# Attention of a two-layer decoder trunk: half of each unit's softmax scaling as row-scalar products on GpSimd

## The chip, the cores and the metric

One core of one Trainium2 chip. The metric is the device time of one launch in microseconds; of the kernel before there are three runs, with a median of 1051.75 us (1051.14 to 1052.2). Engines are called by their short names in the profile: PE (TensorE; PEld is its weight load), DVE (VectorE), ACT (ScalarE), POOL (GpSimd) and SP (the queue that issues most transfers).

## The reference

Layer one is a gated MLP with a spatial mix inside chunks of 128 positions. It also yields one K and one V for the second layer, which is attention over a sliding window of 128 positions, with 16 query heads that share 4 key/value heads, a sink logit per head and a linear position bias (cut to what the change touches):

```
logits = einsum('btkgd,bskd->bkgts', qb, kb) + alibi
logits = where(valid, logits, -inf)
m      = maximum(max(logits, -1), sink)
p      = exp(logits - m)
denom  = sum(p, -1) + exp(sink - m)
o      = einsum('bkgts,bskd->btkgd', p, vb) / denom
y      = (o * silu(z)) @ w_out
```

Every array is float32: x is (1, 1024, 1024), there are 8 blocks of 128 positions, and heads are 64 wide.

## The kernel before, in words

Large products are made in three passes: each operand is split into a rounded part `hi` and a rest `lo`, and PE adds hi*hi, hi*lo and lo*hi (L169 to L171). For a weight of the second layer, ACT makes `whi` (L109, or L105) and DVE makes `wlo` (L110, or L106) from a raw tile that a transfer has brought; `whi` and `wlo` have two buffers each. A weight that carries a gain is split in two halves, k=0 and then k=1, and PE's product reads the half that it needs.

Attention runs over the 1024 positions in two halves of 512 (`attn(0)`, `attn(1)`). Each half has 8 *units*, one for each pair of key/value heads p (0 or 1) and each block b of 128 positions; a unit has eight heads. In this text "unit 5_0" is block 5, pair 0. A unit goes through these steps:

- `scores(gp)`, for the first four heads (gp=0) and then for the last four (gp=1): eight matmuls (L1050) into two banks of PSUM; on DVE a predicated copy per bank (L1055) that folds the window, and one custom operation per head (L1061) that adds the bias and leaves the row's extreme in `mx`; on ACT one exponential per head (L1065) that leaves the row sum in `dn`.
- `normalise`: one reciprocal of `dn` for eight heads (L1070) and one multiplication of all eight heads' probabilities `pr` by it (L1071), both on DVE.
- `transposes`: PE transposes the eight heads of `pr` (L1078), ACT copies them to `pc` (L1079), POOL cuts the two triangles of the window out of it with two selects (`pp` L1082, `pc` L1083; a sequence's first block has only the second).
- `values`: PE multiplies `pc` and `pp` with V (L1097, L1099), DVE multiplies by the gate z (L1103) and splits the result (L105, L106).

The loop of `attn` staggers the units: in step i stand the scores of the first four heads of unit i, the values of unit i-2, the transposes of unit i-1, the scores of the last four heads of unit i and its normalisation. Between these, `more()` lets PE do pieces of other work: the products for K, V, q and z of the second half (`qz`, `pk`, `pv`) beside `attn(0)`, and the rest of z and the output product of the first half (`ob`) beside `attn(1)`. When a group of four q products is complete, ACT and DVE empty its four banks (L971 and L972, two halves per bank), and the banks are then used again.

Within an engine the instructions run in one fixed order. A list scheduler sets it when the kernel is built, from the program's order and its own estimate of when operands are ready, so a change at one place can move neighbours too.

Of the kernel before, what the change touches and what calls it, by code (L numbers as in the profile page):

```python
# [12 lines left out]
ALU = mybir.AluOpType  # L13

P = 128
# [35 lines left out]
def tile_yoco(  # L51
# [19 lines left out]
    nc = tc.nc  # L71
# [9 lines left out]
    def bank(tag, name):  # L81
        return psum.tile([P, 512], F32, tag=tag, name=name)
# [425 lines left out]
    def uz_layer():  # L508
# [149 lines left out]
        for q in range(len(quads) + 1):  # L658
# [39 lines left out]
            if zz:  # L698
                spatial(g, 0, 0)
                spatial(g, 0, 1)  # L700
                if not last:
                    finish(g, 0, 0)
            else:
                normalise(g)
# [22 lines left out]
    def post_gain(src, name):  # L727
        g = const.tile([P, D], F32, tag="gpost", name=name)
        nc.sync.dma_start(out=g, in_=src.partition_broadcast(P))
        return g  # L730
# [291 lines left out]
    class Unit:  # L1022
# [6 lines left out]
        def scores(self, gp):  # L1029
            b, p, q = self.b, self.p, self.q  # L1030
            bs_ = slice((b % 4) * P, (b % 4 + 1) * P)
            w0 = 0 if b > 0 else P
            if gp == 0:
                pr = bp.tile([P, 1088], F32, tag="pr", name=f"pr{self.id}", bufs=2)
                self.pr = pr = pr[:, 0:8 * (P + 1)].rearrange("p (a b) -> p a b", a=8)
                self.mx = bp.tile([P, 8], F32, tag="mx", name=f"mx{self.id}", bufs=2)
                self.dn = bp.tile([P, 8], F32, tag="dn", name=f"dn{self.id}", bufs=2)
                nc.vector.tensor_copy(pr[:, :, P].rearrange("p (c a b) -> p c a b", c=2, a=2),
                                      snk[:, 2 * p:2 * p + 2].rearrange("p a (c b) -> p c a b", c=2))
            pr, mx, dn = self.pr, self.mx, self.dn  # L1040
            pss = []
            for par in range(2):
                pss.append(bank("s", f"s{self.id}_{gp}{par}").rearrange("p (g s) -> p g s", g=2))
            ks = slice(b * P - P + w0, (b + 1) * P)

            for g in range(2):
                m = p * 4 + gp * 2 + g
                for par in range(2):
                    for k, w in enumerate((kh, kl)):
                        nc.tensor.matmul(pss[par][:, g, w0:256], lhsT=q[par][:, m, bs_], rhs=w[par][:, p, ks],  # L1050
                                         start=g + k == 0, stop=g + k == 2, skip_group_check=True)
            for par in range(2):
                ps = pss[par]
                c = ps[:, :, P:256]
                nc.vector.copy_predicated(c, mrg.bitcast(U32).unsqueeze(1).broadcast_to([P, 2, P]),  # L1055
                                          ps[:, :, 0:P] if b > 0 else neg.unsqueeze(1).broadcast_to([P, 2, P]))
                kv = 2 * p + par
                for g in range(2):
                    gg = 2 * gp + g
                    i = 4 * gp + 2 * par + g  # L1060
                    nc.vector.tensor_tensor_reduce(pr[:, i, 0:P], c[:, g], bias[:, gg], -(4.0 ** -kv),  # L1061
                                                   snk[:, kv, gg:gg + 1], ALU.add, ALU.min, mx[:, i:i + 1])

            for i in range(4 * gp, 4 * gp + 4):
                nc.scalar.activation(pr[:, i], pr[:, i], AF.Exp, bias=mx[:, i:i + 1], scale=-1.0,  # L1065
                                     accum_out=dn[:, i:i + 1])

        def normalise(self):
            dn, pv = self.dn, self.pr[:, :, 0:P]
            nc.vector.reciprocal(dn, dn)  # L1070
            nc.vector.tensor_tensor(pv, pv, dn.unsqueeze(2).broadcast_to([P, 8, P]), ALU.mult)  # L1071

        def transposes(self):
            self.pc = pc = st.tile([P, 8, P], F32, tag="xt", name=f"pc{self.id}")
# [136 lines left out]
    gp = post_gain(b_post, "gpb")  # L1211
# [82 lines left out]
```

## Time and profile before

| | us |
|---|---|
| median of the runs | 1051.75 |
| the profiled execution's own time | 1051.56 |
| its span | 1049.8 |
| outside its span | 1.76 |
| PE busy | 1039.2 |
| DVE busy | 731.9 |
| ACT busy | 577.2 |
| POOL busy | 195.2 |

The span is the time from the program's first to its last instruction on the profiled core; the execution's own time is longer by what lies around it. In timelines a row holds start, duration, engine, line, operation, the tiles written and read, shapes, the count of merged instructions, and in brackets the idle time before the row and what ended it.

### The profile page before, as it was taken

To read this page: it belongs to the slowest core of one execution; us is meant where nothing else is said; L and a number is where in the kernel's file an instruction comes from. 1 tells how busy PE (TensorE), PEld (TensorE's weight loads), DVE (VectorE), ACT (ScalarE), POOL (GpSimd) and SP (SyncE) were. 2 spreads that over 40 slices of the span, in tenths; PEclk is the share of its full clock that TensorE was granted. 3 is DMA by queue.
4 is the path that set the end of the run, shared out by engine and by line. 5 is a ranking of instruction groups with operands and counts; after the bars stand their busy time and mean duration, and the time that the engine had idled before them with its cause. 6 is when DMAs were issued, how large, how long until landed. Compare 5 with 4: busy or idle time off the path is not lost.

```text
span 1049.8 us, 13661 instructions
## 1 busy us (share of the span) xinstructions
PE 1039.2 (99%) x4994; PEld 854.8 (81%) x4994; DVE 731.9 (70%) x1244; ACT 577.2 (55%) x989; POOL 195.2 (19%) x153
## 2 busy tenths in 40 slices
PE   9999999999999999999999999999999999999997
PEld 7888788888888888888888888888888777877776
DVE  6997466867768668677697587665247776667763
ACT  6683444555465565555444464654466665786631
POOL 0300003253342542530200000100001111011120
PEclk9999999999999999999999999999999999999999
DMA  8877252334333333347897642532222121211363
GB/s 310 271 282 269 101 177 88 116 105 143 124 121 116 132 124 117 108 137 272 322 352 270 201 160 93 200 102 86 95 81 71 51 81 61 81 61 61 121 220 120
DMA packets 80899, 157.56 MB, mean 150 GB/s; under 512 B 5824, under 2 KB 32704, under 8 KB 80832
## 3 DMA queue, kind: packets, MB, share of 16 engines
q1 hardware_dynamic: 76176, 147.75, 41.2%
q10 hardware_dynamic: 4656, 8.94, 2.4%
q8 instruction: 39, 0.64, 0.3%
q14 instruction: 28, 0.23, 0.1%
HBM read 125.21 MB, written 31.46 MB: 149 GB/s over the span
## 4 chain that ended last, share of the span: by engine, by line
PE 93%; DVE 4%; ACT 1%; issue 0%; DMA 0%; POOL 0%; DVEq 0%; POOLq 0%; ACTq 0%
PE ob L169 6%; PE ub L169 6%; PE ub L171 6%; PE ob L171 6%; PE ob L170 6%; PE ub L170 6%; PE qz L169 5%; PE qz L171 5%; PE qz L170 5%; PE uc L169 3%; PE uc L171 3%; PE uc L170 3%; PE s L1050 3%; PE sp L614 3%; PE vb L170 2%; PE vb L171 2%
## 5 line engine op out<-in xcount | busy, mean ns | idle before, releaser
L110 DVE SCALAR_TENSOR_TENSOR wlo<-raw_w,gn,whi 128x512 fp32r<-128x512 f32 x80 | 58.7, 758 | 62.2 <-ACT whi L109 62.0
L169 PE MATMUL qz<-n_hi,whi 128*128 128x512 f32 x256 | 101.0, 394 | 0.4 <-DVE q_lo L972 0.4
L171 PE MATMUL qz<-n_hi,wlo 128*128 128x512 f32 x256 | 100.0, 391 | 1.2 <-DVE wlo L110 1.2
L170 PE MATMUL qz<-n_lo,whi 128*128 128x512 f32 x256 | 99.8, 390 | 0.0
L109 ACT ACTIVATE whi<-raw_w,gn 128x512 fp32r<-128x512 f32 x80 | 54.9, 716 | 54.2 <-PE qz L170 35.0
L1065 ACT ACTIVATE pr<-pr,mx 128x129 f32<-128x129 f32 x128 | 50.0, 393 | 40.1 <-DVE mx L1061 40.0
L169 PEld LDWEIGHTS qz<-n_hi,whi 128*128 128x128 f32 x256 | 48.0, 188 | 16.6 <-issue 6.5
L105 ACT ACTIVATE uzhilo_g<-f 128x1024 fp32r<-128x1024 f32 x31 | 32.9, 1060 | 48.6 <-PE uc L171 42.7
L171 PEld LDWEIGHTS qz<-n_hi,wlo 128*128 128x128 f32 x256 | 48.0, 188 | 12.3 <-DVE wlo L110 2.1
L170 PEld LDWEIGHTS qz<-n_lo,whi 128*128 128x128 f32 x256 | 48.1, 188 | 9.3
L106 DVE TENSOR_TENSOR uzhilo_g<-f,uzhilo_g 128x1024 fp32r<-128x1024 f32 x31 | 39.0, 1257 | 19.9 <-ACT uzhilo_g L105 19.9
L209 ACT ACTIVATE uz_slots<-ub 128x512 f32<-128x512 f32 x48 | 28.3, 590 | 42.4 <-PE ub L171 39.0
L169 PE MATMUL ub<-T,whi_g 128*128 128x512 f32 x128 | 50.7, 396 | 0.0
L169 PE MATMUL ub<-T,uzhilo_g 128*128 128x512 f32 x128 | 50.5, 395 | 0.0
L171 PE MATMUL ub<-T,wlo_g 128*128 128x512 f32 x128 | 49.9, 390 | 0.0
L171 PE MATMUL ub<-T,uzhilo_g 128*128 128x512 f32 x128 | 49.9, 390 | 0.0
L170 PE MATMUL ub<-T,uzhilo_g 128*128 128x512 f32 x128 | 49.8, 389 | 0.0
L170 PE MATMUL ub<-T,whi_g 128*128 128x512 f32 x128 | 49.8, 389 | 0.0
L169 PE MATMUL uc<-T,uzhilo_g 128*128 128x512 f32 x124 | 48.9, 395 | 0.0
L170 PE MATMUL uc<-T,uzhilo_g 128*128 128x512 f32 x124 | 48.3, 389 | 0.0
L171 PE MATMUL uc<-T,uzhilo_g 128*128 128x512 f32 x124 | 48.3, 389 | 0.0
L105 ACT ACTIVATE whi_g<-raw_uz 128x1024 fp32r<-128x1024 f32 (+1 forms) x31 | 26.5, 854 | 36.7 <-PE ub L170 15.6
(332 smaller groups left out, 3071.4 us busy)
## 6 DMA issues: line engine op xcount, KB each, us to landing
raw_uz<-in_wuz_in_dram SPq DMA_DIRECT2D x32, 512.0 KB, 3.4
raw_w<-in_wqz_dram SPq DMA_DIRECT2D x32, 512.0 KB, 3.5
td<-uz_slots SPq DMA_DIRECT2D x56, 256.0 KB, 2.2
orawP2a<-td SPq DMA_DIRECT2D x28, 512.0 KB, 4.0
raw<-in_wv_in_dram SPq DMA_DIRECT2D x17, 512.0 KB, 4.8
vg<-vd SPq DMA_DIRECT2D x8, 1024.0 KB, 5.4
orawP2b<-in_wo_a_dram SPq DMA_DIRECT2D x16, 512.0 KB, 7.7
vraw<-in_wv_in_dram SPq DMA_DIRECT2D x13, 512.0 KB, 4.4
```

Of the source, the lines that this page charges most:

```text
L105: nc.scalar.activation(hi, src, AF.Copy)
L106: nc.vector.tensor_tensor(lo, src, hi.bitcast(F32), ALU.subtract)
L109: nc.scalar.activation(hi, src, AF.Copy, scale=g)
L110: nc.vector.scalar_tensor_tensor(lo, src, g, hi.bitcast(F32), ALU.mult, ALU.subtract)
L169: nc.tensor.matmul(out, lhsT=a_hi, rhs=b_hi, start=start, stop=False, skip_group_check=True)
L170: nc.tensor.matmul(out, lhsT=a_hi, rhs=b_lo, start=False, stop=False, skip_group_check=True)
L171: nc.tensor.matmul(out, lhsT=a_lo, rhs=b_hi, start=False, stop=stop, skip_group_check=True)
L209: nc.scalar.activation(out, a, AF.Copy)
L614: nc.tensor.matmul(psv[:, n], lhsT=d["vg"][:, 4 * j + n, i * P:(i + 1) * P], rhs=d["wc"], start=True, stop=True)
L1050: nc.tensor.matmul(pss[par][:, g, w0:256], lhsT=q[par][:, m, bs_], rhs=w[par][:, p, ks], start=g + k == 0, stop=g + k == 2, skip_group_che ...
L1065: nc.scalar.activation(pr[:, i], pr[:, i], AF.Exp, bias=mx[:, i:i + 1], scale=-1.0, accum_out=dn[:, i:i + 1])
```

## The change

After the scores of the last four heads are issued, a reciprocal of the first four heads' sums is made on DVE (new L1053), and four POOL instructions each multiply one head's 128x128 probabilities by its column of `dn`, in place (new L1055). `normalise` (now L1070 to L1075) does the last four heads alone, as one reciprocal of four columns and one multiplication of four heads. All lines behind the new ones are four higher than before.

```
+            if gp == 1:
+                nc.vector.reciprocal(dn[:, 0:4], dn[:, 0:4])
+                for i in range(4):
+                    nc.gpsimd.tensor_scalar(pr[:, i, 0:P], pr[:, i, 0:P], dn[:, i:i + 1], None, ALU.mult)
...
         def normalise(self):
-            dn, pv = self.dn, self.pr[:, :, 0:P]
+            dn, pv = self.dn[:, 4:8], self.pr[:, 4:8, 0:P]
             nc.vector.reciprocal(dn, dn)
-            nc.vector.tensor_tensor(pv, pv, dn.unsqueeze(2).broadcast_to([P, 8, P]), ALU.mult)
+            nc.vector.tensor_tensor(pv, pv, dn.unsqueeze(2).broadcast_to([P, 4, P]), ALU.mult)
```

The new order differs from the old at several places on DVE and ACT, and on PE at one: of the eight score matmuls of the first four heads of unit 3_0, four now stand behind twelve `qz` matmuls instead of ahead of them.

The first place to look at is DVE behind the normalisation of unit 0_1, where four banks of q products (`qz1_0_0` to `qz1_0_3`) are emptied; `q1_hi` and `q1_lo` are the two halves written from a bank, `s1_1` are the next unit's scores. Before:

```order
L1070 RECIPROCAL dn0_1_6367<-dn0_1_6367 128x8
L1071 TENSOR_TENSOR pr0_1_6365<-pr0_1_6365,dn0_1_6367 128x8x128
L972 SCALAR_TENSOR_TENSOR q1_hi_5837<-qz1_0_1_6208,qsc_4951,q1_hi_5837 64x512
L972 SCALAR_TENSOR_TENSOR q1_hi_5837<-qz1_0_2_6209,qsc_4951,q1_hi_5837 64x512
L972 SCALAR_TENSOR_TENSOR q1_hi_5837<-qz1_0_3_6210,qsc_4951,q1_hi_5837 64x512
L972 SCALAR_TENSOR_TENSOR q1_lo_5838<-qz1_0_1_6208,qsc_4951,q1_lo_5838 64x512
L972 SCALAR_TENSOR_TENSOR q1_lo_5838<-qz1_0_2_6209,qsc_4951,q1_lo_5838 64x512
L972 SCALAR_TENSOR_TENSOR q1_lo_5838<-qz1_0_3_6210,qsc_4951,q1_lo_5838 64x512
```

The same place in the changed kernel:

```order
L1074 RECIPROCAL dn0_1_6387<-dn0_1_6387 128x4
L1075 TENSOR_TENSOR pr0_1_6385<-pr0_1_6385,dn0_1_6387 128x4x128
L972 SCALAR_TENSOR_TENSOR q1_hi_5837<-qz1_0_1_6223,qsc_4951,q1_hi_5837 64x512
L972 SCALAR_TENSOR_TENSOR q1_hi_5837<-qz1_0_2_6224,qsc_4951,q1_hi_5837 64x512
L1059 COPY_PREDICATED s1_1_00_6524<-mrg_4944,s1_1_00_6524 128x2x128
L972 SCALAR_TENSOR_TENSOR q1_lo_5838<-qz1_0_1_6223,qsc_4951,q1_lo_5838 64x512
L972 SCALAR_TENSOR_TENSOR q1_hi_5837<-qz1_0_3_6225,qsc_4951,q1_hi_5837 64x512
L972 SCALAR_TENSOR_TENSOR q1_lo_5838<-qz1_0_2_6224,qsc_4951,q1_lo_5838 64x512
L1065 ISA pr1_1_6520,mx1_1_6521<-s1_1_00_6524,bias_4942,snk_4953 128x128
L1065 ISA mx1_1_6521 128x1
L972 SCALAR_TENSOR_TENSOR q1_lo_5838<-qz1_0_3_6225,qsc_4951,q1_lo_5838 64x512
```

The multiplication ahead of the eviction is half as wide, the last operation on the bank `qz1_0_1` has moved one place up against the other evictions, and one predicated copy and one custom operation of unit 1_1 now stand among them. ACT's order has the matching swap (its half of `qz1_0_1` ahead of its half of `qz1_0_3`).

The second place is DVE at the scores of the last four heads of unit 4_0 (`s4_0_10`, `s4_0_11`), between the two halves of the weight split `wlo37`. Before:

```order
L110 SCALAR_TENSOR_TENSOR wlo37_7048<-raw_w37_6947,gn_80,whi37_7047 128x4x128
L1055 COPY_PREDICATED s4_0_10_7073<-mrg_4944,s4_0_10_7073 128x2x128
L1055 COPY_PREDICATED s4_0_11_7074<-mrg_4944,s4_0_11_7074 128x2x128
L110 SCALAR_TENSOR_TENSOR wlo37_7048<-raw_w37_6947,gn_80,whi37_7047 128x4x128
L1061 ISA pr4_0_7019,mx4_0_7020<-s4_0_10_7073,bias_4942,snk_4953 128x128
```

In the changed kernel:

```order
L110 SCALAR_TENSOR_TENSOR wlo37_7088<-raw_w37_6987,gn_80,whi37_7087 128x4x128
L1059 COPY_PREDICATED s4_0_10_7113<-mrg_4944,s4_0_10_7113 128x2x128
L1053 RECIPROCAL dn4_0_7061<-dn4_0_7061 128x4
L1059 COPY_PREDICATED s4_0_11_7114<-mrg_4944,s4_0_11_7114 128x2x128
L110 SCALAR_TENSOR_TENSOR wlo37_7088<-raw_w37_6987,gn_80,whi37_7087 128x4x128
L1065 ISA pr4_0_7059,mx4_0_7060<-s4_0_10_7113,bias_4942,snk_4953 128x128
```

The new reciprocal, which releases the four products on POOL, stands two instructions ahead of the second half of `wlo37`.

The third place is POOL from unit 4_0 to unit 6_0. Before, it holds the selects alone:

```order
L1082 AFFINE_SELECT pp4_0_7184<-pc4_0_7171 128x1024
L1083 AFFINE_SELECT pc4_0_7171<-pc4_0_7171 128x1024
L1082 AFFINE_SELECT pp5_0_7300<-pc5_0_7287 128x1024
L1083 AFFINE_SELECT pc5_0_7287<-pc5_0_7287 128x1024
L1082 AFFINE_SELECT pp6_0_7413<-pc6_0_7400 128x1024
L1083 AFFINE_SELECT pc6_0_7400<-pc6_0_7400 128x1024
```

In the changed kernel:

```order
L1055 TENSOR_SCALAR pr4_0_7059<-pr4_0_7059,dn4_0_7061 128x128 x4
L1055 TENSOR_SCALAR pr5_0_7166<-pr5_0_7166,dn5_0_7168 128x128 x4
L1086 AFFINE_SELECT pp4_0_7229<-pc4_0_7216 128x1024
L1087 AFFINE_SELECT pc4_0_7216<-pc4_0_7216 128x1024
L1055 TENSOR_SCALAR pr6_0_7277<-pr6_0_7277,dn6_0_7279 128x128 x4
L1086 AFFINE_SELECT pp5_0_7350<-pc5_0_7337 128x1024
L1087 AFFINE_SELECT pc5_0_7337<-pc5_0_7337 128x1024
L1055 TENSOR_SCALAR pr7_0_7405<-pr7_0_7405,dn7_0_7407 128x128 x4
L1086 AFFINE_SELECT pp6_0_7468<-pc6_0_7455 128x1024
L1087 AFFINE_SELECT pc6_0_7455<-pc6_0_7455 128x1024
```

Four products of a unit now stand ahead of the two selects of the unit before it, so a select can wait for products that came first.

## The prediction

> **What bounds the kernel now.** I read the page's first lines, then the stretch in which attention runs, then what PE waited for. The columns of the second row are length, then busy time and count for each engine.
>
> ```profile
> span 1049.8 us, 13661 instructions
> PE 1039.2 (99%) x4994; PEld 854.8 (81%) x4994; DVE 731.9 (70%) x1244; ACT 577.2 (55%) x989; POOL 195.2 (19%) x153
> ...
> 769.00:1005.00 236.00, 235.56 (x1251) 184.46 (x1250) 170.42 (x485) 157.62 (x418) 36.14 (x32) 1.00 0.23 72
> ...
> PE qz L169 <- DVE q_lo L972: 0.4, 1, 0.4
> ```
>
> PE is busy in 1039.2 of 1049.8 us, and in the 236 us from 769 to 1005, which hold every instruction that the change touches, it is idle for 236.00 - 235.56 = 0.44 us. That is one wait, for DVE's `q_lo` (L972). The change takes no matmul away, and PE's granted clock is already 1.00 there. So the most that it can gain is 0.44 us, 0.04%. About 0.2%, 2.1 us, is what a measurement of this kernel can tell from no change. The question is only whether the change makes PE wait.
>
> **What is removed and what is added.** Rows by line (count, then busy us and mean ns), then rows of single instructions:
>
> ```profile
> L1071 DVE TENSOR_TENSOR pr<-pr,dn 128x1024 f32<-128x1024 f32 x16 | 19.6, 1224 | 0.5
> 920.59 0.68 DVE L106 TENSOR_TENSOR q_lo<-z,q_hi 128x512 fp32r<-128x512 f32 x1
> L586 POOL TENSOR_SCALAR_AFFINE_SELECT wc<-wc x8: 292/298/8106, 38.9 to 412.0; 128x128 f32<-128x128 f32 x8
> L1284 POOL MEMSET const-float32-0.0<- 128x1 f32 x1 | 0.1, 103 | 0.3 <-issue 0.3
> L206 POOL TENSOR_TENSOR f<-raw_uz 128x512 f32<-128x512 f32 x15 | 20.1, 1338 | 127.6 <-DMA raw_uz<-in_wuz_in_dram 85.5 <-DVE uzhilo_g L106 42.1
> ```
>
> DVE loses half of sixteen multiplications: 1.22 us becomes about 0.68, the duration of a multiplication-like operation on 512 columns with both inputs in SBUF. That frees 16 x 0.54 = 8.6 us of DVE. Sixteen more reciprocals at 0.20 us (first row below) give 3.2 back. None of this is on PE's path except where PE waits for DVE. POOL gains 64 products of 128x128, which this trace does not have. Its nearest row is the select of the same shape with one input, 0.298 us at the median; the far ends are 0.10 us, a memset of one column, and 1.34 us, an addition on four times the columns. I take 0.30, with the gap of 0.07 that stands between two selects below: four products take 4 x 0.30 + 3 x 0.07 = 1.4 us.
>
> **The one wait goes.** DVE's rows at the first place that the change's section shows, then one of ACT's, then the matmuls of PE that begin in the last three of the four banks:
>
> ```profile
> 831.98 0.20 DVE L1070 RECIPROCAL dn<-dn 128x8 f32<-128x8 f32 x1 [0.91 <-ACT pr L1065]
> 832.21 1.22 DVE L1071 TENSOR_TENSOR pr<-pr,dn 128x1024 f32<-128x1024 f32 x1
> 833.47 2.06 DVE L972 SCALAR_TENSOR_TENSOR q_hi<-qz,qsc,q_hi 64x512 fp32r<-64x512 f32 x3
> 835.56 0.76 DVE L972 SCALAR_TENSOR_TENSOR q_lo<-qz,qsc,q_lo 64x512 fp32r<-64x512 f32 x1
> 838.06 0.76 DVE L1055 COPY_PREDICATED s<-mrg,s 128x256 f32<-128x256 uint32 x2
> ...
> 833.73 0.67 ACT L971 ACTIVATE q_hi<-qz,qsc 64x512 fp32r<-64x512 f32 x1
> ...
> 836.47 0.48 PE L169 MATMUL qz<-n_hi,whi 128*128 128x512 f32 x1 [0.45 <-DVE q_lo L972]
> 837.93 0.39 PE L169 MATMUL qz<-n_hi,whi 128*128 128x512 f32 x1
> 839.29 0.39 PE L169 MATMUL qz<-n_hi,whi 128*128 128x512 f32 x1
> ```
>
> PE could have started at 836.02 and waited until the bank was emptied at 836.32. Afterwards the multiplication ends about 0.54 us sooner (832.9). Behind it stand two `q_hi` (0.69 each, to 834.3), one predicated copy (0.38, to 834.7) and the `q_lo` of this bank (0.76, to 835.4). ACT's half of that bank now stands where 833.73 is, ends at 834.4 and is not late. 835.4 is ahead of 836.02 by 0.6, so the 0.44 us goes. By the same count (one more `q_hi`, one custom operation, two `q_lo`) the two next banks are free at 836.8 and 838.0, and PE, 0.45 earlier than now, takes them at 837.5 and 838.8.
>
> **The new wait of the transposes is covered.** PE's transposes now wait for POOL as well. Two units have the shortest cover, 0_0 and 4_0: the sum of the fourth exponential, and the transposes, of each.
>
> ```profile
> 774.49 0.19 ACT L1065 ACTIVATION_READ_ACCUMULATOR pr<-pr,mx 128x1 f32 x1
> 785.78 0.49 PE L1078 MATMUL pt<-ident,pr 128*128 128x128 f32 x3
> 900.48 0.19 ACT L1065 ACTIVATION_READ_ACCUMULATOR pr<-pr,mx 128x1 f32 x1
> 909.87 0.38 PE L1078 MATMUL pt<-ident,pr 128*128 128x128 f32 x2
> ```
>
> From 900.67 to 909.87 are 9.2 us for a reciprocal and 1.4 us of products; unit 0_0 has 11.1, and the others have more. The reciprocal, which waits for ACT, holds back DVE's queue only until the four exponentials are done. In most units it stands behind the gate's multiplication, when they are; in units 0_0, 1_0 and 5_0 it stands right behind the custom operations, where DVE idles anyway for ACT's next `whi`. I cost this at nothing.
>
> **Who is queued behind the products.** On POOL these are the selects. The tightest pair that shares the queue with products that come just before is that of unit 6_0:
>
> ```profile
> 935.76 0.18 DVE L1038 COPY pr<-snk 128x8 f32<-128x8 f32 x1 [2.43 <-PE pt L1078]
> 937.50 1.09 POOL L1082 TENSOR_SCALAR_AFFINE_SELECT pp<-pc 128x1024 f32<-128x1024 f32 x1 [8.97 <-ACT pc L1079]
> 938.66 1.96 POOL L1083 TENSOR_SCALAR_AFFINE_SELECT pc<-pc 128x1024 f32<-128x1024 f32 x1
> 941.64 0.66 PE L1097 MATMUL o<-pc,vt 128*64 128x512 f32 x2
> 926.28 1.09 POOL L1082 TENSOR_SCALAR_AFFINE_SELECT pp<-pc 128x1024 f32<-128x1024 f32 x1 [12.31 <-ACT pc L1079]
> 927.44 1.09 POOL L1083 TENSOR_SCALAR_AFFINE_SELECT pc<-pc 128x1024 f32<-128x1024 f32 x1
> 928.59 0.66 PE L1097 MATMUL o<-pc,vt 128*64 128x512 f32 x2
> ```
>
> Unit 7_0's reciprocal stands behind the copy that ends at 935.94, so products run from 936.2 to 937.6, and the selects start 0.1 later than now. Their result is ready at 940.62 and used at 941.64; that 1.0 us holds. Unit 5_0's selects have only 0.06 us (928.53 to 928.59), but the products ahead of them (reciprocal behind the `q_lo` of 920.59) are through by 922.8, and their own start is set by ACT. Cost nothing; 0.87 if one of those selects is stretched as the one at 938.66 was (1.96 for 1.09).
>
> **DVE and POOL get in each other's way.** Two selects on POOL and a weight split on DVE:
>
> ```profile
> 881.33 1.09 POOL L1082 TENSOR_SCALAR_AFFINE_SELECT pp<-pc 128x1024 f32<-128x1024 f32 x1 [9.36 <-ACT pc L1079]
> 882.49 1.09 POOL L1083 TENSOR_SCALAR_AFFINE_SELECT pc<-pc 128x1024 f32<-128x1024 f32 x1
> 890.07 1.41 DVE L110 SCALAR_TENSOR_TENSOR wlo<-raw_w,gn,whi 128x512 fp32r<-128x512 f32 x2 [1.46 <-ACT whi L109]
> 882.49 2.30 DVE L110 SCALAR_TENSOR_TENSOR wlo<-raw_w,gn,whi 128x512 fp32r<-128x512 f32 x2 [1.78 <-ACT whi L109]
> L110 DVE SCALAR_TENSOR_TENSOR wlo<-raw_w,gn,whi x38: 701/745/1636, 769.7 to 910.4; 128x512 fp32r<-128x512 f32 x38
> ```
>
> Two splits take 1.41 us at 890.07, with POOL idle; at 882.49 they take 2.30. The 0.89 more is most of the select that ran beside the first. The custom operations, which read PSUM, show no such rows. In the Trainium skill, "SBUF — State Buffer", section "Who interferes with whom", it is said that a DVE instruction with two SBUF inputs and a GpSimd instruction that reads SBUF exclude each other for a whole instruction, whichever starts first; this trace agrees (1.636 us against 0.745), and by that rule a split would lose at most one product, 0.30 us, per meeting, if DVE gets the turn after it.
>
> The place where it could count is the second half of `wlo37`:
>
> ```profile
> 900.68 0.76 DVE L1055 COPY_PREDICATED s<-mrg,s 128x256 f32<-128x256 uint32 x2 [2.55 <-PE s L1050]
> 901.35 0.75 DVE L110 SCALAR_TENSOR_TENSOR wlo<-raw_w,gn,whi 128x512 fp32r<-128x512 f32 x1
> 903.24 0.39 PE L171 MATMUL qz<-n_hi,wlo 128*128 128x512 f32 x1
> ```
>
> It ends at 902.10, and the first matmul that reads this half (k=1) starts at 903.24: 1.14 us of margin. The reciprocal takes 0.20. It releases the products at about 901.3, so the split, due at 901.55, meets the first: no more than 0.3 lost if DVE gets the next turn, and the cost is 0. If POOL keeps its turn for all four, the split runs from 902.7 to 903.45, and PE waits 0.2. I take 0.
>
> **The sum.** Against the profiled execution: 1051.56 - 0.44 + 0 = 1051.1; the runs' median lies 0.19 above it, so 1051.75 - 0.44 = 1051.3.
>
> **Rivals.**
>
> *POOL keeps its turn.* As worked out, +0.2 at `wlo37`: 1051.5, with a stretched select at 928.59 (+0.87) 1052.4. For it speaks that at 882.49 POOL went from one select to the next while DVE came in. Against it, that DVE arrived with that second select, not before. 0.09.
>
> *Slow products: slower.* If a product with a scalar from SBUF costs what POOL's two-input addition does, 1.34 us, four take 5.6. At unit 6_0 the products then end at 941.8 and the selects (2.25) at 944.1, and PE, at 941.64, waits 2.5. With the split behind four products (901.3 + 5.6 + 0.75 = 907.65 against 903.24) PE waits 4.4. In all +2.5 to +6.9: 1053.8 to 1058.2. It begins where a product is over (941.64 - 936.2 - 0.2 - 2.3) / 4 = 0.73 us. For it: the change has a second operand, and additions here cost over four times the select's 0.3. Against it: the scalar is one value per row, and an addition at 1.34 has four times the columns. 0.05.
>
> *The first product is slow.* The first select of its kind took 8.1 us (the maximum in L586's row). Unit 0_0's products would start at about 775.0 and end by 784.2, and its transposes start at 785.78. The unit's next rows on DVE, and one from beside that slow select:
>
> ```profile
> 776.44 0.75 DVE L110 SCALAR_TENSOR_TENSOR wlo<-raw_w,gn,whi 128x512 fp32r<-128x512 f32 x1 [3.16 <-ACT whi L109]
> 780.77 1.23 DVE L1071 TENSOR_TENSOR pr<-pr,dn 128x1024 f32<-128x1024 f32 x1
> 40.00 1.22 DVE L106 TENSOR_TENSOR T<-tch,T 128x1024 fp32r<-128x1024 f32 x1
> ```
>
> That is hidden, unless DVE is shut out meanwhile: the split at 776.44 would then start 6.7 us late, at 783.1, the normalisation, now through at 782.0, would end at 788.1 (its half takes 0.54 less), and PE would wait 2.3 us from 785.78: 1053.6. Against it: during the slow select (38.9 to 47.0) DVE did its two-input work in the usual 1.22. The Trainium skill, "GPSIMD Engine Reference", section "Instruction dispatch", puts the first call of a freshly loaded kernel at about 6 us. 0.03.
>
> **How the numbers follow.** Forecast 0.82, the rivals 0.09, 0.05 and 0.03, the rest 0.01. The first rival is within 0.2% too, so: same 0.90, slower 0.08, faster 0.02 (the bound of 0.44 leaves only the spread of the runs). The range is 1051.14 - 0.44 = 1050.7 for the lowest run with the whole gain, and up to 1052.4, the first rival with its stretched select; it leaves out the two slow rivals.
>
> **What would show it.** PE's idle time from 769 to 1005 falls from 0.44 to about 0, with no wait by `qz` L169 on `q_lo`; PE's busy time is as before. The products take 0.3 us each. Transposes and values show no wait on POOL. DVE's busy time falls by about 5 us, with some L110 and L106 stretched by 0.3. A row in PE's waits that names `pr` L1055, `pc` L1087 or `wlo` L110 inside attention, or a product over 0.73 us, would make it wrong.

## The result, and the profile after

The changed kernel takes 1052.68 us (median of 20 runs, 1051.86 to 1053.2), the kernel before, run beside it, 1051.32 us (20 runs, 1050.28 to 1052.2). The ratio is 1.0014, 95% interval 1.0007 to 1.002: slower by 0.14%, which is inside the 0.2% that the prediction called no change, but 0.3 us above the upper end of its range.

The page of the changed kernel: its first lines, then the row of the stretch from 769 to 1005 us (length, then busy time and count of PE, PEld, DVE, ACT and POOL).

```profile
span 1050.5 us, 13763 instructions
...
PE 1039.3 (99%) x4994; PEld 854.8 (81%) x4994; DVE 727.8 (69%) x1260; ACT 578.1 (55%) x989; POOL 247.5 (24%) x217
...
769.00:1005.00 236.00, 234.56 (x1245) 183.67 (x1244) 166.60 (x500) 157.79 (x418) 84.29 (x96) 1.00 0.23 72
```

DVE is 4.1 us less busy than before (731.9), POOL 52.3 us more (195.2). PE has as much work as before, but in the stretch of attention it is idle for 236.00 - 234.56 = 1.44 us, where it was idle for 0.44. The two waits of PE inside attention (us in total, times, longest):

```profile
PE o L1101 <- POOL pc L1087: 1.0, 1, 1.0
...
PE qz L169 <- DVE kl L1019: 0.4, 1, 0.4
```

The wait for `q_lo` L972 is gone; two others came. To place them, follow the same four groups of matmuls through both kernels: the transposes of unit 0_0, later transposes, those of unit 4_0, and the values near 1003 us. Start, duration, engine, line; first the kernel before.

```profile
785.78 1.03 PE L1078 MATMUL pt<-ident,pr 128*128 128x128 f32 x8
...
812.66 1.04 PE L1078 MATMUL pt<-ident,pr 128*128 128x128 f32 x8
...
909.87 1.04 PE L1078 MATMUL pt<-ident,pr 128*128 128x128 f32 x8
...
1002.78 1.08 PE L1097 MATMUL o<-pc,vt 128*64 128x512 f32 x4
```

Then the changed kernel:

```profile
785.31 1.03 PE L1082 MATMUL pt<-ident,pr 128*128 128x128 f32 x8
...
812.85 1.04 PE L1082 MATMUL pt<-ident,pr 128*128 128x128 f32 x8
...
909.39 1.04 PE L1082 MATMUL pt<-ident,pr 128*128 128x128 f32 x8
...
1003.41 1.08 PE L1101 MATMUL o<-pc,vt 128*64 128x512 f32 x4
```

The three distances are 26.88, 97.21 and 92.91 us before, and 27.54, 96.54 and 94.02 us after: **+0.66**, **-0.67** and **+1.11**, together +1.10 us. The medians differ by 1.36, which agrees within the interval (0.7 to 2.1 us). These three distances are read in every experiment below, from the one trace of each kernel, because they show tenths of a microsecond that medians of whole runs do not.

The -0.67 is the wait at 836.47, which the prediction expected to go. The +0.66 is here. First the kernel before, PE and then DVE:

```profile
803.20 0.28 PE L1050 MATMUL s<-kh,q_hi 128*128 128x256 f32 x1
803.31 0.39 PE L169 MATMUL qz<-n_hi,whi 128*128 128x512 f32 x1
803.54 0.40 PE L170 MATMUL qz<-n_lo,whi 128*128 128x512 f32 x1
...
802.29 0.69 DVE L1019 TENSOR_TENSOR kl<-pk,kh 64x512 fp32r<-64x512 f32 x1
```

And the changed kernel:

```profile
802.25 0.28 PE L1050 MATMUL s<-kh,q_hi 128*128 128x256 f32 x1
802.93 0.49 PE L169 MATMUL qz<-n_hi,whi 128*128 128x512 f32 x1 [0.40 <-DVE kl L1019]
803.26 0.39 PE L170 MATMUL qz<-n_lo,whi 128*128 128x512 f32 x1
...
802.18 0.69 DVE L1019 TENSOR_TENSOR kl<-pk,kh 64x512 fp32r<-64x512 f32 x1
```

Before, five score matmuls of unit 3_0 stood ahead of this `qz` matmul; now one does. PE reaches it sooner by four steps of about 0.12 us (802.72 to 803.20 before), while DVE is still emptying a bank of keys until 802.87. The 0.40 us that the profile calls idle understates the place: from the score to the second `qz` matmul it is now 803.26 - 802.25 = 1.01 us, before it was 803.54 - 803.20 = 0.34, so 0.67 us are lost. (A row lasts longer than the step to the next row, 0.28 us against 0.11 here, and idle time counts from the row's end.) DVE is later, too. Counted from the first transposes, the emptying began at 16.51 us and the `qz` matmul at 17.53 before (802.29 and 803.31, less 785.78); now they begin at 16.87 and 17.62.

The +1.11 is where the prediction saw a margin of 1.0 us, at the selects of unit 6_0 behind the products of unit 7_0. The changed kernel's POOL, DVE and PE:

```profile
935.85 3.78 POOL L1055 TENSOR_SCALAR pr<-pr,dn 128x128 f32<-128x128 f32 x4 [7.79 <-DVE dn L1053]
939.59 1.09 POOL L1086 TENSOR_SCALAR_AFFINE_SELECT pp<-pc 128x1024 f32<-128x1024 f32 x1
940.75 1.49 POOL L1087 TENSOR_SCALAR_AFFINE_SELECT pc<-pc 128x1024 f32<-128x1024 f32 x1
...
937.93 1.22 DVE L106 TENSOR_TENSOR wlo<-raw_w,whi 128x1024 fp32r<-128x1024 f32 x1
...
940.59 0.69 DVE L1075 TENSOR_TENSOR pr<-pr,dn 128x512 f32<-128x512 f32 x1
...
942.29 1.09 PE L1101 MATMUL o<-pc,vt 128*64 128x512 f32 x4 [1.04 <-POOL pc L1087]
...
L1055 POOL TENSOR_SCALAR pr<-pr,dn x64: 598/607/1974, 774.5 to 988.4; 128x128 f32<-128x128 f32 x64
```

Four products take 3.78 us where the prediction had 1.4. The last row (shortest, median, longest, in ns) says why in part: a product is 0.607 us at the median, twice the 0.30 assumed. Four of those are 2.43 us; the other 1.35 us is a stretch beside DVE's two-input work, the split at 937.93 above all: the four take 0.61, 1.08, 0.60 and 1.56 us, and the last began at 938.07. The last select is stretched too, 1.49 for 1.09, beside the multiplication at 940.59.

### The profile page after: what moved, and what is told of

Read it like the earlier page. It is cut to its first block, busy times and chain, and to the rows that moved or that the text cites. A ratio compares the mean times of both kernels' runs of the same rounds, so it can differ in the third digit from the quotient of the medians.

```text
span 1050.5 us, 13763 instructions
## 1 busy us (share of the span) xinstructions
PE 1039.3 (99%) x4994; PEld 854.8 (81%) x4994; DVE 727.8 (69%) x1260; ACT 578.1 (55%) x989; POOL 247.5 (24%) x217
## 4 chain that ended last, share of the span: by engine, by line
PE 92%; DVE 4%; DMA 1%; ACT 1%; issue 1%; POOL 1%; SPq 0%; DVEq 0%; POOLq 0%; ACTq 0%
PE ub L169 6%; PE ub L171 6%; PE ub L170 6%; PE ob L169 5%; PE qz L169 5%; PE ob L170 5%; PE ob L171 5%; PE qz L171 5%; PE qz L170 5%; PE uc L171 3%; PE uc L169 3%; PE uc L170 3%; PE sp L614 3%; PE s L1050 3%; PE vb L170 2%; PE vb L169 2%
## 5 line engine op out<-in xcount | busy, mean ns | idle before, releaser
L110 DVE SCALAR_TENSOR_TENSOR wlo<-raw_w,gn,whi 128x512 fp32r<-128x512 f32 x80 | 59.1, 762 | 59.0 <-ACT whi L109 58.7
L1055 POOL TENSOR_SCALAR pr<-pr,dn 128x128 f32<-128x128 f32 x64 | 48.7, 778 | 206.8 <-DVE dn L1053 206.8
L106 DVE TENSOR_TENSOR uzhilo_g<-f,uzhilo_g 128x1024 fp32r<-128x1024 f32 x31 | 38.6, 1245 | 19.9 <-ACT uzhilo_g L105 19.9
L206 POOL TENSOR_TENSOR f<-raw_uz 128x512 f32<-128x512 f32 x15 | 20.1, 1338 | 127.4 <-DMA raw_uz<-in_wuz_in_dram 90.3
L206 POOL TENSOR_TENSOR f<-raw_uz,raw_uz 128x512 f32<-128x512 f32 x15 | 19.2, 1283 | 128.2 <-DVE uzhilo_g L106 128.2
L169 PE MATMUL uc<-T,uzhilo_g 128*128 128x512 f32 x124 | 48.9, 395 | 0.0
```

What stands on the lines that cost most here:

```text
L106: nc.vector.tensor_tensor(lo, src, hi.bitcast(F32), ALU.subtract)
L110: nc.vector.scalar_tensor_tensor(lo, src, g, hi.bitcast(F32), ALU.mult, ALU.subtract)
L169: nc.tensor.matmul(out, lhsT=a_hi, rhs=b_hi, start=start, stop=False, skip_group_check=True)
L206: (eng or nc.vector).tensor_tensor(out, a, b, op)
L1055: nc.gpsimd.tensor_scalar(pr[:, i, 0:P], pr[:, i, 0:P], dn[:, i:i + 1], None, ALU.mult)
```

## The experiments

Theory A takes the three places for the whole story: +0.66 from a changed order at 803, +1.11 from GpSimd's queue at 942, -0.67 at 836. Theory B is a general one: GpSimd's work gets in DVE's way everywhere, and the kernel pays for the amount. Theory C: the early reciprocal holds DVE's queue, and GpSimd has nothing to do with it. Theories and rivals with other letters are named in the expectation of the run that tests them. All kernels were timed with the kernel before on the same chip; ratios have intervals of about 0.0009 either way, or 0.9 us (0.0013 for every product twice, with 4 runs in place of 11), so medians alone separate 1.4 from 0 but hardly 0.6 from 0. Distances are start to start of the four groups above, and "sum" is their change against the 217.00 us of before.

| Kernel (us) | first (803) | second (836) | third (942) | sum | median less before's |
|---|---|---|---|---|---|
| before | 26.88 | 97.21 | 92.91 | 0 | 0 |
| changed | 27.54 | 96.54 | 94.02 | +1.10 | +1.36 |
| unit 1_0 old | 26.88 | 96.54 | 94.04 | +0.46 | +0.16 |
| unit 7_0 old | 27.49 | 96.54 | 92.90 | -0.07 | +0.08 |
| units 1_0 and 7_0 old | 26.88 | 96.55 | 92.89 | -0.68 | -0.62 |
| products issued late | 27.52 | 96.56 | 92.89 | -0.03 | +0.46 |
| unit 0_1 alone | 26.88 | 96.56 | 92.92 | -0.64 | -0.86 |
| unit 1_0 alone | 27.54 | 97.22 | 92.92 | +0.68 | +0.73 |
| products by 1.0 | 27.51 | 96.54 | 92.92 | -0.03 | +0.08 |
| one wide product | 27.54 | 96.52 | 92.92 | -0.02 | -0.31 |
| every product twice | 27.51 | 100.12 | 99.43 | +10.06 | +8.10 |
| early half on DVE | 27.53 | 97.06 | 92.92 | +0.51 | +0.49 |
| one two-input product | 27.53 | 96.54 | 92.90 | -0.03 | +0.04 |
| no products | 27.51 | 96.53 | 92.92 | -0.04 | +0.27 |
| two-input, unit 1_0 old | 26.87 | 96.56 | 92.90 | -0.67 | -0.53 |
| late, unit 1_0 old | 26.88 | 96.56 | 92.92 | -0.64 | -0.53 |

The table is read by columns: apart from two kernels (every product twice, and the early half on DVE), each place has just two values, within 0.05 us.

### Two units put back, one at a time and together

```
-            if gp == 1:
+            if gp == 1 and (b, p) not in ((1, 0), (7, 0)):
...
-            dn, pv = self.dn[:, 4:8], self.pr[:, 4:8, 0:P]
+            lo = 0 if (self.b, self.p) in ((1, 0), (7, 0)) else 4
+            dn, pv = self.dn[:, lo:8], self.pr[:, lo:8, 0:P]
...
```

The multiplication in `normalise` covers heads `lo` to 7. The other two kernels have one of the pair in that list. Unit 1_0 old:

> Only unit 1_0 goes back to the old path (all eight heads normalised on DVE); this puts TensorE's order back to that of the kernel before, with the four score matmuls of unit 3_0 ahead of the qz matmuls of bank 1_0_2. Theory A (two new waits of TensorE, one behind the products of unit 7_0 and one from the changed order of the matmuls, less the old wait that went): the wait of 0.40 us on DVE L1019 near 803 us is gone, the one of 1.04 us on POOL L1087 near 942 us stays; 0.7 us faster than the changed kernel, so about 0.7 us slower than the kernel before. Theory B (GpSimd's work slows DVE's and so everything a little, in all sixteen units): one unit of sixteen, 0.1 us faster than the changed kernel, 1.3 us slower than before. Theory C (the reciprocal that now stands ahead in DVE's queue holds what follows): as B, 1.3 us slower than before.

Unit 7_0 old:

> Only unit 7_0 goes back to the old path; TensorE's order stays that of the changed kernel. Theory A: the wait on POOL L1087 near 942 us is gone, the one on DVE L1019 near 803 us stays; 1.1 us faster than the changed kernel, so about 0.3 us slower than before. Theories B and C: one unit of sixteen, 0.1 us faster than the changed kernel, 1.3 us slower than before.

Both old:

> Units 1_0 and 7_0 both on the old path, the other fourteen as changed. Theory A: both new waits gone and the old one near 836 us still away; 1.8 us faster than the changed kernel, 0.4 us faster than before. Theories B and C: 0.2 us faster than the changed kernel, 1.2 us slower than before.

Measured ratios: 1.0004 (0.9995 to 1.0013), 1.0002 (0.9993 to 1.0011) and 0.9994 (0.9985 to 1.0002). PE's wait in attention with unit 1_0 old, then with unit 7_0 old, then the whole stretch with both old:

```profile
PE o L1102 <- POOL pc L1088: 1.1, 1, 1.1
```

```profile
PE qz L169 <- DVE kl L1019: 0.4, 1, 0.4
```

```profile
769.00:1005.00 236.00, 236.00 (x1254) 185.03 (x1253) 167.95 (x499) 158.24 (x418) 78.07 (x88) 1.00 0.23 72
```

Each unit takes away its own wait and leaves the other's, and with both back PE is busy for all of the 236 us. B and C wanted 0.1 us for a unit of sixteen; the distances moved by 0.64 and 1.17. It is the distances that decide: the interval with unit 1_0 old reaches 1.0013, 1.4 us, which holds A's 0.7 and B's 1.3.

### All products kept, issued later

```
-            if gp == 1:
-                nc.vector.reciprocal(dn[:, 0:4], dn[:, 0:4])
-                for i in range(4):
-                    nc.gpsimd.tensor_scalar(pr[:, i, 0:P], pr[:, i, 0:P], dn[:, i:i + 1], None, ALU.mult)
...
         def normalise(self):
             dn, pv = self.dn[:, 4:8], self.pr[:, 4:8, 0:P]
-            nc.vector.reciprocal(dn, dn)
+            nc.vector.reciprocal(self.dn, self.dn)
+            for i in range(4):
+                nc.gpsimd.tensor_scalar(self.pr[:, i, 0:P], self.pr[:, i, 0:P], self.dn[:, i:i + 1], None, ALU.mult)
```

> All sixteen units keep their four products on GpSimd, but reciprocal and products are issued where the other four heads are normalised, after the unit's last exponentials; in GpSimd's queue the products of unit 7_0 then stand behind the selects of unit 6_0. GpSimd's busy time stays. TensorE's order is that of the changed kernel. Theory A: the wait near 942 us goes, the one near 803 us stays; 1.1 us faster than the changed kernel, 0.3 us slower than before; the transposes of every unit still have about 9 us of cover. Theory B: GpSimd does as much as in the changed kernel, so 1.4 us slower than before. Theory C: DVE's queue has its old order again, so all of the loss goes: as before.

Ratio 1.0006 (0.9997 to 1.0014). POOL, and PE at the values of unit 6_0:

```profile
937.73 1.09 POOL L1084 TENSOR_SCALAR_AFFINE_SELECT pp<-pc 128x1024 f32<-128x1024 f32 x1 [4.40 <-ACT pc L1081]
938.89 1.96 POOL L1085 TENSOR_SCALAR_AFFINE_SELECT pc<-pc 128x1024 f32<-128x1024 f32 x1
941.42 2.84 POOL L1072 TENSOR_SCALAR pr<-pr,dn 128x128 f32<-128x128 f32 x4 [0.57 <-DVE dn L1070]
...
941.86 1.09 PE L1099 MATMUL o<-pc,vt 128*64 128x512 f32 x4
```

GpSimd does as much as in the changed kernel, but unit 7_0's products come behind the selects, which are done at 940.85, 1.0 us ahead of PE. The third distance is that of before: the place in the queue counted, not the amount, against B. C had the whole loss go, but the first distance stays at 27.52.

### One unit alone

The kernel before with one unit's first four heads on GpSimd. The diff of unit 0_1 (`lo` in `normalise` has the same list); the other names `(1, 0)`.

```
-            if gp == 1:
+            if gp == 1 and (b, p) not in [(bb, pp) for bb in range(8) for pp in range(2) if (bb, pp) != (0, 1)]:
...
```

Unit 0_1 alone:

> Only unit 0_1 has its first four heads normalised by products on GpSimd, the other fifteen units are as before; TensorE's order is that of the kernel before. Theory A: the gain is in this one unit: DVE is done with half a multiplication earlier ahead of the q evictions that TensorE waited for near 836 us; that wait goes, no other comes: 0.6 us faster than before. Rival: the gain comes from DVE's lighter load in the units ahead too (2.3 us of busy time over sixteen units), so one unit brings 0.1 us or less and the wait of 0.4 us near 836 us stays.

Ratio 0.9992 (0.9984 to 1.0001). Attention:

```profile
769.00:1005.00 236.00, 236.00 (x1253) 185.01 (x1252) 170.87 (x486) 158.13 (x418) 39.27 (x36) 1.00 0.22 72
```

One unit of sixteen gives all the gain that the change has. Unit 1_0 alone:

> Only unit 1_0 has its first four heads normalised by products on GpSimd, the other fifteen units are as before. TensorE's order is that of the changed kernel: four score matmuls of unit 3_0 stand behind the qz matmuls of bank 1_0_2. Theory A, first form: the order alone makes the wait of 0.4 us on DVE L1019 near 803 us, worth 0.65 us; the old wait near 836 us stays, since unit 0_1 is as before: 0.65 us slower than before. Second form: TensorE comes later to the q evictions near 836 us, DVE is done by then, and that wait goes: as before, 0.0 us. Rival: the wait near 803 us needs DVE's changed load in the units ahead of it: no wait there, as before.

Ratio 1.0006 (0.9998 to 1.0015). PE's two waits in attention:

```profile
PE qz L169 <- DVE q_lo L972: 0.5, 1, 0.5
PE qz L169 <- DVE kl L1019: 0.4, 1, 0.4
```

The first form holds: both waits stand, each at its price, and PE's coming later at 803 does not hide the wait at 836. One unit moves the order of four matmuls elsewhere and costs as much as another gains.

### What a product costs

The products by the number 1.0 in place of the row scalar (the first four heads are not normalised):

```
-                    nc.gpsimd.tensor_scalar(pr[:, i, 0:P], pr[:, i, 0:P], dn[:, i:i + 1], None, ALU.mult)
+                    nc.gpsimd.tensor_scalar(pr[:, i, 0:P], pr[:, i, 0:P], 1.0, None, ALU.mult)
```

> The four products of each unit multiply by the number 1.0 in place of the row scalar, so the first four heads are not normalised. Theory D (the row scalar makes the product twice as long as the select of 0.30 us): a product takes 0.30 us, unit 7_0's four are done 1.2 us earlier, the wait near 942 us goes; 1.0 us faster than the changed kernel, 0.4 us slower than before. Theory E (a multiplication of 128x128 costs GpSimd 0.6 us whatever the second factor): 0.60 us each, the wait of 1.0 us stays, time as the changed kernel, 1.4 us slower than before.

One product over four heads, all by the first head's scalar, so three heads have the wrong scale:

```
-                for i in range(4):
-                    nc.gpsimd.tensor_scalar(pr[:, i, 0:P], pr[:, i, 0:P], dn[:, i:i + 1], None, ALU.mult)
+                nc.gpsimd.tensor_scalar(pr[:, 0:4, 0:P], pr[:, 0:4, 0:P], dn[:, 0:1], None, ALU.mult)
```

> One GpSimd multiplication over four heads (128x512) by the row scalar of the first head in place of four over 128x128; heads two to four get the wrong scale. Theory E1 (most of 0.6 us is a price per instruction): about 0.9 us for the one instruction, unit 7_0's work on GpSimd is over 1.4 us or more earlier, the wait near 942 us goes; 1.0 us faster than the changed kernel, 0.4 us slower than before. Theory E2 (the price goes by elements): 2.4 us for the one, the wait stays, 1.4 us slower than before.

One multiplication with two inputs, the four denominators repeated along their heads:

```
-                for i in range(4):
-                    nc.gpsimd.tensor_scalar(pr[:, i, 0:P], pr[:, i, 0:P], dn[:, i:i + 1], None, ALU.mult)
+                nc.gpsimd.tensor_tensor(pr[:, 0:4, 0:P], pr[:, 0:4, 0:P],
+                                        dn[:, 0:4].unsqueeze(2).broadcast_to([P, 4, P]), ALU.mult)
```

> One GpSimd multiplication of four heads (128x512) by the four denominators, each repeated along its head, in place of four products: two inputs, not one with a scalar. Theory E1: as the 128x512 with one scalar (1.57 us), and as GpSimd's own tensor_tensor rows of 128x512 (1.3 to 1.6 us); the wait near 942 us goes, the one near 803 us stays: 0.0 to 0.3 us slower than before. Rival H (DVE's two-input work and GpSimd's stand in each other's way for a whole instruction, so one long instruction is worse than four short ones): the instruction takes 3 us or more at unit 7_0, the wait near 942 us stays, 1.4 us slower than before.

Ratios 1.0001 (0.9992 to 1.001), 0.9998 (0.9989 to 1.0006) and 0.9999 (0.999 to 1.0008). The instruction's row in each, and what POOL did at unit 7_0. By 1.0:

```profile
L1055 POOL TENSOR_SCALAR pr<-pr x64: 527/532/1562, 774.0 to 986.4; 128x128 f32<-128x128 f32 x64
...
935.20 2.02 POOL L1055 TENSOR_SCALAR pr<-pr 128x128 f32<-128x128 f32 x4 [6.33 <-ACT pr L1069]
937.83 1.09 POOL L1086 TENSOR_SCALAR_AFFINE_SELECT pp<-pc 128x1024 f32<-128x1024 f32 x1 [0.61 <-ACT pc L1083]
938.99 1.96 POOL L1087 TENSOR_SCALAR_AFFINE_SELECT pc<-pc 128x1024 f32<-128x1024 f32 x1
```

One wide product, with the last select behind it:

```profile
L1054 POOL TENSOR_SCALAR pr<-pr,dn x16: 1566/1569/2892, 774.7 to 983.8; 128x512 f32<-128x512 f32 x16
...
938.74 1.96 POOL L1086 TENSOR_SCALAR_AFFINE_SELECT pc<-pc 128x1024 f32<-128x1024 f32 x1
```

One two-input product:

```profile
L1054 POOL TENSOR_TENSOR pr<-pr,dn x16: 1039/1040/1858, 775.1 to 984.5; 128x512 f32<-128x512 f32 x16
...
936.39 1.04 POOL L1054 TENSOR_TENSOR pr<-pr,dn 128x512 f32<-128x512 f32 x1 [7.77 <-DVE dn L1053]
937.59 1.35 POOL L1086 TENSOR_SCALAR_AFFINE_SELECT pp<-pc 128x1024 f32<-128x1024 f32 x1 [0.15 <-ACT pc L1083]
939.00 1.96 POOL L1087 TENSOR_SCALAR_AFFINE_SELECT pc<-pc 128x1024 f32<-128x1024 f32 x1
```

Theory D falls: without the row scalar a product still takes 0.53 us. E is nearly right about the price, 0.53 for 0.60, and wrong about the wait, which went: these products need no reciprocal and start 0.95 us ahead of DVE's copy L1038 (936.15), where the changed kernel's start 0.50 behind it (935.35), and they are over at 937.22, before DVE's split of 938.74, so nothing stretches them. For the wide product E1 was nearer, though 1.57 us is more than the 0.9 that it gave: (1.569 - 0.607) / 384 columns is 2.5 ns a column, which leaves an estimated 0.29 us per instruction. Rival H falls: the two-input product is the cheapest form of all, 1.04 us for four heads against 2.43, and nothing waits at 942. DVE does pay, as H has it: the same work keeps it busy for 171.7 us of the stretch of attention, 166.6 in the changed kernel, but PE does not wait for that. In all three the last select is still stretched, to 1.96, and PE does not wait. So the wait in the changed kernel needs the group's length; a stretched select alone is inside the margin.

### More work, less work, and the same work on DVE

Every product followed by a second one, by 1.0:

```
+                    nc.gpsimd.tensor_scalar(pr[:, i, 0:P], pr[:, i, 0:P], 1.0, None, ALU.mult)
```

> Each product is followed by a second one by 1.0 on the same tile, so GpSimd does eight per unit and 128 in all. Theory A: only unit 7_0's place counts: its group takes 2.4 us longer ahead of the selects of unit 6_0, so the wait near 942 us grows from 1.0 to about 3.4 us, and no other wait of TensorE comes (the transposes had 9 us or more of cover); 2.4 us slower than the changed kernel, 3.8 us slower than before. Theory B (GpSimd's work beside DVE's slows the kernel everywhere): the loss of 1.4 us doubles, 2.8 us slower than before, and the wait near 942 us grows by less than 2 us.

No products, the reciprocal alone (the first four heads are not normalised):

```
-                for i in range(4):
-                    nc.gpsimd.tensor_scalar(pr[:, i, 0:P], pr[:, i, 0:P], dn[:, i:i + 1], None, ALU.mult)
```

> The early reciprocal stays, the four products are left out, so the first four heads are not normalised; DVE multiplies the other four. TensorE's order is that of the changed kernel. Theory A: no wait near 942 us, the one near 803 us stays, none near 836 us: 0.0 to 0.3 us slower than before. Theory C (the early reciprocal holds DVE's queue): the products never mattered, 1.4 us slower than before.

The early multiplication on DVE:

```
-                for i in range(4):
-                    nc.gpsimd.tensor_scalar(pr[:, i, 0:P], pr[:, i, 0:P], dn[:, i:i + 1], None, ALU.mult)
+                nc.vector.tensor_tensor(pr[:, 0:4, 0:P], pr[:, 0:4, 0:P],
+                                        dn[:, 0:4].unsqueeze(2).broadcast_to([P, 4, P]), ALU.mult)
```

> The early multiplication of the first four heads stays where the change put it, but DVE does it, in one instruction over four heads; GpSimd does only its selects. TensorE's order is that of the changed kernel. Theory A: the wait near 942 us is GpSimd's and goes, the one near 803 us stays, the one near 836 us stays away since half of unit 0_1's multiplication is done early: 0.0 to 0.3 us slower than before. Rival G (the gain near 836 us needs DVE to be relieved): the wait near 836 us comes back, 0.7 us slower than before. Theory C (the early reciprocal holds DVE's queue, not GpSimd): 1.4 us slower than before.

Ratios 1.0083 (1.0069 to 1.0096), 1.0003 (0.9994 to 1.0012) and 1.0005 (0.9996 to 1.0014). With every product doubled, PE's waits for the selects in total, then the three, and one of the matmuls behind the first of them:

```profile
PE o L1102 <- POOL pc L1088: 6.7, 3, 3.2
...
849.82 1.59 PE L1102 MATMUL o<-pc,vt 128*64 128x512 f32 x4 [1.95 <-POOL pc L1088]
...
851.93 0.63 PE L170 MATMUL qz<-n_lo,whi 128*128 128x512 f32 x1
...
948.70 1.50 PE L1102 MATMUL o<-pc,vt 128*64 128x512 f32 x4 [3.19 <-POOL pc L1088]
...
1001.89 1.08 PE L1102 MATMUL o<-pc,vt 128*64 128x512 f32 x4 [1.52 <-POOL pc L1088]
```

The wait at 942 grew to 3.2, as A had it, but A was wrong that no other comes: two more selects were queued behind products with less room than a doubling takes, and 3.8 became 8.1. B's 2.8 is further off. All three waits are of the one kind, values that wait for a select. The margin is a property of the place in GpSimd's queue, and there are several places. But the waits are only 6.7 of the 10.06 us. Behind the first two of them PE's granted clock is 0.72 (849 to 855 us) and 0.57 (949 to 953), and a matmul that takes 0.39 us elsewhere takes 0.63; PE is busy for 1043.0 us in all, 3.7 more than in the changed kernel with as many matmuls. Behind the wait of 1.52, and behind the 1.04 of the changed kernel, the clock stays at 1.00. So a longer wait cost more than its length here. (This trace is of the longest of the four runs, 1061.85 us; the others took 1059.7 to 1059.8.)

Without products the early reciprocal costs nothing at 942, so C falls there. The wait at 803 needs no GpSimd work, as the first distance of 27.51 shows, and no early reciprocal either: the late products had 27.52. With the half on DVE the place at 942 is clear and the wait at 836 goes, but another eviction is late instead:

```profile
872.16 0.47 PE L169 MATMUL qz<-n_hi,whi 128*128 128x512 f32 x1 [0.26 <-DVE q_lo L972]
```

Rival G wanted 0.7 us and the wait of 836 back; it is 0.49 us and a wait 36 us further on.

### Both waits avoided, nearly all products kept

The two-input product, and the late products, each with unit 1_0 on the old path (the conditions are those of the first diff). The first:

> Fifteen units have their first four heads normalised by one GpSimd multiplication of two inputs (1.04 us at its shortest), unit 1_0 is as before, which keeps TensorE's order of before. Theory A: no wait near 803, 836 or 942 us, TensorE busy for the whole of 769 to 1005 us: 0.6 us faster than before. Rival I (the gain of 0.6 us with two kernels was the noise of medians): as before, 0.0 us, and a wait in one of the three places.

The second:

> Fifteen units keep the four products on GpSimd, issued after the unit's last exponentials and so behind the selects of the unit ahead; unit 1_0 is as before, which keeps TensorE's order of before. GpSimd is as busy as in the changed kernel, less one unit's products. Theory A: no wait near 803, 836 or 942 us: 0.6 us faster than before. Theory B (what GpSimd does beside DVE costs by its amount): 1.3 us slower than before. Rival I: as before, 0.0 us.

Ratios 0.9995 (0.9986 to 1.0004) and 0.9994 (0.9986 to 1.0003). Attention in the first, and in the second:

```profile
769.00:1005.00 236.00, 236.00 (x1251) 184.95 (x1251) 171.11 (x500) 158.42 (x419) 53.58 (x47) 1.00 0.22 72
```

```profile
769.00:1005.00 236.00, 236.00 (x1254) 184.97 (x1253) 165.35 (x485) 158.15 (x418) 83.52 (x92) 1.00 0.22 72
```

The second has 83.5 us of GpSimd's work, within 1 us of the changed kernel's 84.3, and no wait. Theory B is out, and the two waits are all of the loss that can be seen. Four kernels now have the gain without the waits: medians 0.62, 0.86, 0.53 and 0.53 us below before's, a mean of 0.64, and distances shorter by 0.64 to 0.68. No single interval excludes 1.0; that four agree with each other and with their distances is what Rival I does not explain, though the last two share their runs of before. With PE busy in 236 of 236 us, this part of the kernel has no more of that kind to give.

## Why the prediction was wrong

- **PE bounds the kernel; the question is whether it has to wait.** Right. The sum that the runs give is -0.67 + 0.66 + 1.11 = +1.10 us in place of -0.44.
- **The wait at 836 goes.** Right, and unit 0_1 alone does it. Its size was off: idle time of 0.44 was read as the most that can be gained, and the place was worth 0.67, as the distances show. Idle time counts from the end of a row, which lasts longer than the step to the next, and the matmul that follows a wait is also slower to hand over to the next one (0.33 us from the first `qz` to the second at 802.93, 0.23 at 803.31 before).
- **A product takes 0.30 us.** Wrong by a factor of two, 0.607. The select of the same shape was chosen for its shape; it was the wrong row, 0.298 us where a multiplication takes 0.53 even by a constant. The rejected row, an addition over 512 columns at 1.34 us, was no better: it would have made four products 5.6 us, and they are 2.43.
- **Unit 6_0's selects cost nothing.** This is the step that failed: +1.11. The margin of 1.0 us and the threshold, 0.73 us per product, were worked out with products that nothing stretches, and 0.607 is below that threshold. The prediction did consider GpSimd and DVE shutting each other out, but only as a loss of DVE or of a select, not of the products. In the changed kernel 21 of the 64 products are longer than 0.62 us. Each of the 21 began while an operation of L106 or L110, which read two tiles in SBUF, was running on DVE; the 16 that met such an operation but had begun before it took their usual 0.60 to 0.61. The Trainium skill, "SBUF — State Buffer", section "Who interferes with whom", has this: whichever of the two is issued first keeps the other out for its whole length. The trace agrees: DVE's split of 937.93 took its usual 1.22 us, and the four products took 1.35 more than their own time. How the 1.04 us of wait divide is an estimate from rows, since no kernel kept the price and removed the stretch. By the price alone the products would have ended at 938.28 and the selects (2.25) at 940.53, ahead of PE, which was ready at 941.25 (942.29 - 1.04). With one select stretched by 0.87, as in the kernels above, it would have been 941.40, or 0.15 late. At the predicted 0.30 us a product and with all stretches as measured it would have been 941.05 (935.85 + 1.2 + 1.35 + 2.25 + 0.40), in time. So price and stretch were both needed, and without the products' stretch most of the wait would not have come.
- **PE's order.** The part on the change named the four score matmuls that moved, and the prediction gave them no price at all: +0.66. They were the cover of PE while DVE emptied a bank. That unit 1_0's new path sets the order is shown by adding it alone and by removing it alone. It need not be an early step: the late products have the wait, too, and what all kernels with it share is unit 1_0's halved multiplication in `normalise`. The price has two parts, by an estimate from the rows at 803: with DVE as early as before, the new order would cost 0.2 us (bank empty at 17.20, `qz` at 17.25 in place of 17.05), and with the old order DVE's delay would cost 0.1 (17.62 for 17.53). Most of the loss needs both. Why DVE is 0.36 us later stays open.
- **Transposes, `wlo37`, the reciprocal.** Right: no transposes waited, no wait at `wlo37`, and the reciprocal cost nothing. DVE's busy time fell by 4.1 us against "about 5".
- **The rivals.** "Slow products" had the mechanism and the place, unit 6_0, but put the beginning too high and the chance at 0.05. "The first product is slow" did not happen: the first group at 774.52 took 2.67 us for four. The 6 us that the Trainium skill gives for the first call of a freshly loaded kernel ("GPSIMD Engine Reference", "Instruction dispatch") do not show there; whether this one was freshly loaded the trace does not say.
- **What would make it wrong** was named: a row with `pc` L1087 in PE's waits. It is there, and so are products over 0.73 us.

## What to carry to other kernels

Where one engine is busy for 99% of a stretch, price a change by the margins of the instructions queued behind it, and work out each margin with the new instructions at their stretched length too, not at their own alone. An order of instructions that moves on the bounding engine is a term of the sum, however few they are: look for what those instructions covered. Distances between the same instructions in two traces resolve tenths of a microsecond, and one unit put back at a time names the place.

## What the hardware showed

On GpSimd the same four heads cost 4 x 0.607 = 2.43 us as products with a row scalar, 1.57 us as one product with a scalar over 512 columns, and 1.04 us as one multiplication of two tiles. The form with two inputs was expected to take as long as the wide product or longer, and it is the cheapest; it needs one instruction for four different scalars. Its second input is four values, each repeated along its head; the two-input operations of L206 on whole tiles of that size took 1.28 us or more at the mean. A select over 1024 columns takes 1.09 us, hardly more than a multiplication over half as many. In the kernel with every product twice, waits of PE of 1.95 and 3.19 us were followed by a granted clock of 0.72 and 0.57 in the next 6 and 4 us; its wait of 1.52 us was not. Why is not tested.
